# Transformer encoder block: prompt scores in tiles of their own, gates and Fourier map around the attention drain re-ordered, three weight splits and two norms moved

## The chip, the cores and the metric

The kernel runs on one core of one Trainium2 chip. The metric is the device time of one execution in microseconds (us). The traces name the engines PE (TensorE), ACT (ScalarE), DVE (VectorE), POOL (GpSimd) and SP (SyncE, which here issues most of the DMAs).

## The reference

One encoder layer in float32 runs on two batches with shared weights: a prompt of 256 tokens and a sample of 1024 tokens. 16 learned meta tokens stand ahead of each.

```python
h = rms_norm(x, norm_mix_g)
z = h @ w_in            # q | k | v | fourier channels | attention gates | fourier gates
q, k = axial_rope(head_rms_norm(q)), axial_rope(head_rms_norm(k))
a  = bidirectional_gqa(q, k, v) @ w_attn_o      # 8 query heads, 2 key/value heads, softmax over all tokens
fo = fourier_mix(f) @ w_four_o                  # real part of a 2-D DFT over positions and channels
merged = sigmoid(g_attn) * a + sigmoid(g_four) * fo
x = x + merged @ w_out
h2 = rms_norm(x, norm_ffn_g)
gate, up = split(h2 @ w_ffn_in)                 # D_FF = 2816
x = x + (silu(gate) * up) @ w_ffn_out
y = rms_norm(x, final_norm_g)                   # meta tokens dropped
```

`D_MODEL` is 1024, the head width 64. Every linear map is wanted at float32 accuracy.

## The kernel before

**Matmuls in three terms.** Each float32 operand is split into a high part (a cast to the short float type `fp32r`) and a low part (the difference). `three` (lines 228 to 234) issues high x high, high x low and low x high, so one product is a triple of matmuls (L232, L233, L234). A weight block is therefore loaded by DMA, cast on ACT and subtracted on DVE or POOL before PE can use it; that is called its split.

**Chunks.** Tokens are kept in three chunks: chunk 0 and 1 are the halves of the sample (512 columns each), chunk 2 the prompt (256). Tiles 0 to 7 are 128 sample tokens each, tiles 8 and 9 are the prompt's.

**Order of work.** `build` opens PSUM pools one after the other and runs: norm, transposes and first gates; Fourier transform in, q, k and v with the gates of chunk 0; attention with the gates of chunks 1 and 2 as filler; merge; `w_out`; SwiGLU in (`ffn_in`); SwiGLU out (`ffn_out`). Inside a `manual_schedule` region the engines named issue in the order in which the code emits the instructions. Attention names PE, ACT, DVE and POOL, the merge PE, ACT and DVE, the second part of `w_out` only PE. Elsewhere, and on SP, a scheduler places instructions. Each engine works through its queue in order.

**Attention.** `attention` goes over 20 units, a tile and a key/value group each, prompt tiles first: `[8, 9] + list(range(8))`. A unit has four heads. Per head: scores into PSUM tile `S` (L1016), the negated row maximum on DVE (L1021), the exponential with row sum on ACT (L1028), the reciprocal on DVE (L1035). `S` is one tile of three banks (1536 columns). A sample head has a new tile; all prompt heads share one, at thirds of 512 columns:

```python
if S is None or t < 8:
    S = ps.tile([P, 1536], F32, tag=tag_s, name=f"S{t}{g}{h}")
base = 248 if t < 8 else (4 * i + h) % 3 * 512
```

The second half of a unit's work, `Second`, follows one unit later in turns, one per block of 128 keys and one for the meta keys (nine turns for the sample, three for the prompt). A turn transposes four heads' probabilities on PE (L916), splits them on ACT (L927) and DVE (L928), and multiplies with the values (`product`, L949 to L954). After the last turn ACT and DVE copy the two halves of `pv` out (L957, L958), POOL adds them (L959), the row sums come by DMA (L960), POOL multiplies (L963) and a DMA stores the result to `a_d` (L966). What is left of the last units after the last score is called the drain.

**The filler.** Attention is a generator that yields each half step of a head with its kind. `Filler` adds `FILL[kind]` ns for each yield to a debt and pulls gate triples from `gate_gen` until it is paid. A triple of n columns costs 3n/2.4: 640 for chunk 1, 320 for chunk 2; there are 12 units of eight triples for each of both chunks. The kinds are "p" for prompt heads, "first" for the first sample unit, "s" for the other sample units, "end" for the last unit and "drain". The splits of the next gate weights and the copies of gate results wait in a list, `later`, for a slack half step.

**Merge.** `merge` goes over eight blocks `i` of 128 output columns. `load` fetches the block's weights, `need` splits them (two sums on DVE, two casts on ACT, two subtractions on DVE: L1163 to L1168), `load_gates` fetches gates, `sigmoid` applies the sigmoid (L1176). `fourier(i)` computes the Fourier map of the block in two halves (`fo`, L1190 and triples), then the sum and the difference of its two PSUM tiles (`fst`, L1203, L1210, L1211) and the products with the gates on POOL (L1220). Then the attention map of the block runs for chunks 0, 2, 1 (`m`). `load_af` loads one chunk of attention results from `a_d` and splits it (L1119, L216, L217). The final cast and subtraction of a chunk's result are put off in the list `late` (`rows`, L1277 and L1278). Loop order before: `fourier(i + 1)`, then `need(i + 2)`, then the chunks of block `i`.

**w_out and SwiGLU.** `w_out` runs for tiles (0, 2, 1, 3, 8, 9) as `w02` and then for (4, 6, 5, 7) as `w1`; the second half of `w1` goes tile by tile. `h2_norm` makes the second norm of a tile (L249, L241, L242, L254), `second_norm` the seven left operands of a pair of tiles. SwiGLU is computed by seven products `j` for each step `e`; `ffn_units` is a generator that loads, adds and splits their weights (L1477 on ACT, L1479 on POOL in the first two steps, on DVE later). Names in the trace: `i` is a SwiGLU product, `A` and `Ah` its left operands, `w` a split weight, `wo` a `w_out` product.

Of the kernel before, what the change touches and what calls it, by code (L numbers as in the profile page):

```python
# [9 lines left out]
F32 = mybir.dt.float32  # L10
# [7 lines left out]
P = 128  # L18
# [34 lines left out]
FINISH = (1, 3, 5, 7, 9)  # L53
LAG = 6000
FIRST = 4
XLOAD = 3
# [103 lines left out]
class Filler:  # L160
# [5 lines left out]
    def __call__(self, cost):  # L166
        self.debt += cost
        while self.live and self.debt > 0:
            try:
                self.debt -= next(self.gen)  # L170
            except StopIteration:
                self.live = False

    def rest(self):
        if self.live:
            run_all(self.gen)

# [6 lines left out]
class Kernel:  # L184
# [379 lines left out]

    FILL = {"s": 550, "p": 150, "first": 1150, "end": 550, "drain": 600}

# [314 lines left out]
    def attention(self, ps, tiles, tag_s, tag_v):  # L881
# [97 lines left out]

        queue, n, divide, S = deque(), 0, None, None  # L980

# [15 lines left out]
        for i, (t, g) in enumerate(units):  # L997
# [10 lines left out]
            for h in range(4):  # L1008
                hq = q[t][:, (4 * g + h) * P : (4 * g + h + 1) * P]

                if S is None or t < 8:
                    S = ps.tile([P, 1536], F32, tag=tag_s, name=f"S{t}{g}{h}")
                base = 248 if t < 8 else (4 * i + h) % 3 * 512
                for lo, hi in zip(cuts, cuts[1:]):
                    for v in range(2):
                        nc.tensor.matmul(  # L1016
                            S[:, base + lo : base + hi], hq, self.kT[seq][g][v][:, lo:hi], start=v == 0, stop=v == 1
                        )
                sm = self.small.tile([P, 4], F32, tag="sm", name="sm", bufs=4)
                nb = sm[:, 0:1]  # L1020
                nc.vector.tensor_reduce(nb, S[:, base : base + L], axis=AX.X, op=ALU.max, negate=True)  # L1021
# [6 lines left out]
                self.last_exp = nc.scalar.activation(  # L1028
                    p[:, :L], S[:, base : base + L], AF.Exp, bias=nb, accum_out=p[:, L:wide]
                )  # L1030
# [17 lines left out]
            queue.append((Second(i, t, g, ps4, slots), n + 1))  # L1048
        divide()
        while queue:  # L1050
            for half in range(2):
# [78 lines left out]
    def merge(self, then):  # L1130
# [46 lines left out]

        def fourier(i):

# [4 lines left out]
            for half in range(2):  # L1184
                pp = []
                for odd in range(2):
                    pm = self.mm[0].tile([P, 512], F32, tag="out", name=f"fo{i}{half}{odd}")
                    if odd == 0:
# [10 lines left out]
                    pp.append(pm)  # L1199
                while late:  # L1200
                    late.popleft()()
                st = sl.get("fst")
# [5 lines left out]
                for l, n, L, b, c0 in spans:  # L1208
# [6 lines left out]
                    for src, t, n in ((x[:, skip:], l + skip - N_META, n - skip), (d[:, m - 1 :: -1], L - (l + m - 1) - N_META, m)):  # L1215
                        while n:
# [4 lines left out]
                            src, t, n = src[:, k:], t + k, n - k  # L1221
                sl.put(st)
            sl.put(w)

# [9 lines left out]
        need(1)  # L1234
        yield from fourier(0)
        load(2)
        load_gates(2)
        for i in range(8):
            yield from fourier(i + 1)
            if i:  # L1240
                need(i + 2)
            if i == 0:
# [50 lines left out]
    def w_out(self, tiles, ps, then=None, apart=False):  # L1293
# [37 lines left out]
        for half in range(2):  # L1331
# [4 lines left out]
            if half and apart:  # L1336
                need(7)
                next(then)
                for ti, t in enumerate(tiles):
                    for kk in range(4):  # L1340
                        product(acc[ti], t, kk, units[4 + kk])
                        yield 1300
                    add(t, half, acc[ti])
                for kk in range(4):
                    sl.put(*units.pop(4 + kk))
                continue
# [140 lines left out]

    def ffn_in(self, ps, units, side, then):
# [4 lines left out]
        ahead = deque()  # L1493

# [9 lines left out]
        for e, (f, chunks) in enumerate(STEPS):  # L1504
# [3 lines left out]
            for j in range(7):  # L1508
                need(AHEAD - (e < N_EARLY))
                w = ahead.popleft()  # L1510
                for c in chunks:
# [45 lines left out]
                    if e < N_EARLY:  # L1557
                        for _ in range(1):
                            next(side, None)
                sl.put(w)  # L1560
# [209 lines left out]
    def build(self):  # L1770
# [3 lines left out]
        with self.psum("pb", {"mm": 4, "tr": 2, "g": 2}) as ps:  # L1774
# [17 lines left out]
            next(gates.gen)  # L1792
        self.M, self.X, self.af = {}, {}, {}
        ps_e = []
# [3 lines left out]
        m = self.merge(w02)  # L1798
        with self.psum("pd", {"S": (1, 1536), "tr": 2, "pv": 1, "g": 2}) as ps:
            E = mybir.EngineType  # L1800
            self.mm = ps, "g"
            with self.tc.manual_schedule(engines={E.PE, E.Activation, E.DVE, E.Pool}):
                later = self.later = deque()
                parts = self.fourier_parts()
                for i, (kind, more, slack) in enumerate(self.attention(ps, [8, 9] + list(range(8)), "S", "pv")):
# [4 lines left out]
                    if kind == "drain" and not self.af:  # L1810
                        next(m)
                        early = chain(self.load_af(0), self.load_af(2))
                        next(early)
                    gates(self.FILL[kind] + more)
                while later:
                    later.popleft()()
                self.later = None
                run_all(parts)
                gates(2600)
                next(m)  # L1820
                self.last_af = self.load_af(1)
                for i, _ in enumerate(early):
                    gates(2600)
                    if i == 0:
                        next(self.last_af)
                gates.rest()
            self.free_hT(self.hT[1])
            self.free_hT(self.hT[2])
        with self.psum("pe", {"in": 4, "out": 4}) as ps:
            self.mm = ps, "in"  # L1830
            ps_e.append(ps)
# [153 lines left out]
```

## Time and profile before

| | us |
|---|---|
| three runs | 1708.84, 1714.28, 1714.66 |
| their median | 1714.28 |
| the profiled execution | 1710.69 |
| its span in the profile | 1708.8 |
| PE busy | 1645.1 |
| DVE busy | 1096.7 |
| ACT busy | 725.4 |
| POOL busy | 355.8 |

The span is that of the profiled execution, from its first to its last instruction; the time of the same execution is 1.9 us longer. Busy times are of the whole span. A busy engine is not one at full speed: the clock granted to PE is shown for each stretch, 1.00 being full. The stages, read from the first and last instruction of the tiles named:

| stage | from | to |
|---|---|---|
| all ahead of attention | 0 | 316.7 |
| prompt attention (first `S` to first sample `S`) | 316.7 | 355.7 |
| sample attention, to the last head's first half step | 355.7 | 622.8 |
| drain, to the last `pv` | 622.8 | 646.5 |
| rest of gates, Fourier map of blocks 0 and 1, chunks 0 and 2 of block 0 | 646.5 | 673.2 |
| merge from block 0, chunk 1 | 673.2 | 757.5 |
| `w_out` | 757.5 | 874.4 |
| start of SwiGLU | 874.4 | 889.7 |
| SwiGLU in and out, final norm | 889.7 | 1708.8 |

### The profile page before, as it was taken

Reading aid. Unit: us, or ns where it says so; the run is one execution under the profiler, and the core shown is the slowest. Engines: PE = TensorE matmul, PEld = TensorE weight load, DVE = VectorE, ACT = ScalarE, POOL = GpSimd, SP = SyncE. Lnnn points to the kernel's source line nnn. Section 1 sums busy time; section 2 is a strip of 40 time slices with the busy share of each in tenths; the row PEclk is TensorE's granted clock in tenths of the full one; section 3 lists DMA queues with packets and bytes.
Section 4 is the critical chain, followed back from the end, with each engine's and each line's share of the span. In section 5 each row is a group of like instructions: output and inputs, shape, how many; then the busy total and the mean of one; then the engine's idle time right before and its main releaser. Section 6 shows DMA issues by size and latency. Waiting matters only on the chain.

```text
span 1708.8 us, 25999 instructions
## 1 busy us (share of the span) xinstructions
PE 1645.1 (96%) x9739; PEld 1479.5 (87%) x9739; DVE 1096.7 (64%) x2028; ACT 725.4 (42%) x1463; POOL 355.8 (21%) x400
## 2 busy tenths in 40 slices
PE   7999999889999998999989999999999999999997
PEld 7888879668888887778879999999999998888886
DVE  5564565357777665651589667666766778765685
ACT  6423233346666665440454222232222224444444
POOL 3451443222234323661451000000000000000002
PEclk9999999899999999999999999999999999999999
DMA  6135221322122246443522222232223237553534
GB/s 248 44 112 191 99 101 61 105 62 70 52 69 64 78 129 225 136 142 111 197 99 90 96 91 73 84 104 92 84 96 100 84 124 258 200 171 98 164 93 154
DMA packets 92453, 198.75 MB, mean 116 GB/s; under 512 B 10230, under 2 KB 41622, under 8 KB 92328
## 3 DMA queue, kind: packets, MB, share of 16 engines
q1 hardware_dynamic: 82296, 179.63, 31.9%
q10 hardware_dynamic: 8400, 12.53, 2.1%
q0 software_dynamic: 1632, 4.93, 0.9%
q8 instruction: 77, 1.26, 0.3%
q14 instruction: 48, 0.39, 0.1%
HBM read 141.58 MB, written 55.47 MB: 115 GB/s over the span
## 4 chain that ended last, share of the span: by engine, by line
PE 75%; DVE 9%; ACT 5%; issue 4%; POOL 3%; DMA 3%; SPq 0%; ACTq 0%; POOLq 0%; DVEq 0%
PE i L234 10%; PE i L232 10%; PE i L233 10%; PE o L234 5%; PE o L233 5%; PE o L232 5%; PE S L1016 4%; PE pt L916 3%; PE g L234 2%; PE g L232 2%; PE g L233 2%; PE pv L949 2%; PE pv L950 1%; PE wo L233 1%; PE wo L234 1%
## 5 line engine op out<-in xcount | busy, mean ns | idle before, releaser
L1477 ACT CAST w<-wi 128x512 fp32r<-128x512 f32 x168 | 104.0, 621 | 270.9 <-PE i L234 217.4
L232 PE MATMUL i<-A,w 128*128 128x384 f32 x616 | 209.0, 339 | 3.0 <-ACT w L1477 2.6
L234 PE MATMUL i<-A,w 128*128 128x384 f32 x616 | 208.9, 340 | 2.3 <-POOL w L1479 2.3
L233 PE MATMUL i<-A,w 128*128 128x384 f32 x616 | 208.5, 338 | 0.0
L234 PE MATMUL i<-Ah,w 128*128 128x256 f32 x616 | 173.3, 282 | 0.0
L233 PE MATMUL i<-Al,w 128*128 128x256 f32 x616 | 173.3, 281 | 0.0
L232 PE MATMUL i<-Ah,w 128*128 128x256 f32 x616 | 173.2, 281 | 0.0
L241 POOL TENSOR_SCALAR fin0r<-fin0ss 128x1 f32<-128x1 f32 x1 | 0.8, 788 | 755.7 <-ACT X L249 755.7
L1479 DVE TENSOR_TENSOR w<-wi,w 128x512 fp32r<-128x512 f32 x154 | 105.2, 684 | 28.7 <-ACT w L1477 28.1
L232 PEld LDWEIGHTS i<-A,w 128*128 128x128 f32 x616 | 116.9, 190 | 3.6 <-ACT w L1477 2.9
L234 PEld LDWEIGHTS i<-A,w 128*128 128x128 f32 x616 | 116.6, 189 | 3.0 <-POOL w L1479 2.9
L233 PEld LDWEIGHTS i<-A,w 128*128 128x128 f32 x616 | 116.7, 189 | 0.0
L232 PEld LDWEIGHTS i<-Ah,w 128*128 128x128 f32 x616 | 116.0, 188 | 0.5 <-ACT w L1477 0.5
L233 PEld LDWEIGHTS i<-Al,w 128*128 128x128 f32 x616 | 116.3, 189 | 0.0
L234 PEld LDWEIGHTS i<-Ah,w 128*128 128x128 f32 x616 | 116.2, 189 | 0.0
L1021 DVE TENSOR_REDUCE sm<-S 128x1 f32<-128x1040 f32 (+1 forms) x80 | 86.4, 1079 | 35.9 <-PE S L1016 33.0
L928 DVE TENSOR_TENSOR pT<-pt,pT 128x512 fp32r<-128x512 f32 x110 | 75.5, 687 | 51.0 <-ACT pT L927 50.9
L916 PE MATMUL pt<-ident,p 128*128 128x128 f32 (+1 forms) x507 | 90.7, 279 | 0.5 <-DVE hT0l L928 0.4
L927 ACT CAST pT<-pt 128x512 fp32r<-128x512 f32 x110 | 64.1, 583 | 49.7 <-PE pt L916 47.1
L234 PE MATMUL o<-wfo,act 128*128 128x512 f32 (+1 forms) x212 | 82.2, 388 | 2.0 <-DVE act L1611 2.0
L233 PE MATMUL o<-wfo,act 128*128 128x512 f32 (+1 forms) x212 | 81.8, 386 | 0.0
L232 PE MATMUL o<-wfo,act 128*128 128x512 f32 (+1 forms) x212 | 81.6, 388 | 0.0
(841 smaller groups left out, 4563.9 us busy)
## 6 DMA issues: line engine op xcount, KB each, us to landing
wi<-w_fi SPq DMA_DIRECT2D x48, 512.0 KB
act_d<-sc SPq DMA_DIRECT2D x77, 192.0 KB
act<-act_d SPq DMA_DIRECT2D x37, 320.0 KB
wg<-w_g SPq DMA_DIRECT2D x23, 512.0 KB
wfo<-w_fo SPq DMA_DIRECT2D x21, 512.0 KB
X<-act_d SPq DMA_DIRECT2D x31, 320.0 KB
act_d<-sc SPq DMA_DIRECT2D x77, 128.0 KB
gt<-gate SPq DMA_DIRECT2D x32, 256.0 KB
```

The source lines that it names most:

```text
L232: mm(out, sh, mh, start=first and i == 0, stop=False)
L233: mm(out, sh, ml, start=False, stop=False)
L234: mm(out, slo, mh, start=False, stop=last and i == n - 1)
L916: nc.tensor.transpose(pt[:m, h * P : (h + 1) * P], me.ps4[h][:, col : col + m], self.ident[:])
L927: nc.scalar.copy(hi, pt[:rows, :])
L928: nc.vector.tensor_tensor(lo, pt[:rows, :], f32(hi), op=ALU.subtract)
L949: nc.tensor.matmul(me.pv[:], vst, pT[:, :512], start=j == 0, stop=False)
L950: nc.tensor.matmul(me.pv[:], vst, pT[:, 512:1024], start=False, stop=False)
L1016: nc.tensor.matmul(S[:, base + lo : base + hi], hq, self.kT[seq][g][v][:, lo:hi], start=v == 0, stop=v == 1)
L1021: nc.vector.tensor_reduce(nb, S[:, base : base + L], axis=AX.X, op=ALU.max, negate=True)
L1477: nc.scalar.copy(w[:, :512], src)
L1479: eng.tensor_tensor(w[:, 512:1024], src, f32(w[:, :512]), op=ALU.subtract)
```

## The change

- **Prompt scores.** The pool of attention has no `S` any more. `attention` opens a pool of its own for scores: three tiles of 512 columns for the prompt, a new tile for each head; when the sample's first head comes it closes that pool and opens one with a tile of 1536. It closes this one before the drain.
- **Filler.** "s" and "end" go from 550 to 660 and "drain" from 600 to 900. In the drain the filler is no longer the gates but the merge generator, up to the end of `fourier(0)`.
- **Preparation.** A generator, `prepare`, starts when the gates have ended: it flushes `later`, frees the transposed inputs `hT[1]` and `hT[2]`, loads weights and gates of block 0 and the attention columns of chunks 0 and 2, and in the next half steps splits them. Before, this began in the drain, and `fourier(0)` after it. The loads and splits of chunk 1 (`last_af`) stay behind the drain.
- **Merge.** `need(i + 2)` runs after the first half of `fourier(i + 1)` instead of after both. The put-off rows come after the sums of a half, not ahead of its copy. Both steps of the first `w_out` weight (load, split) are taken at block 6; before, the split was at block 7.
- **SwiGLU.** In the last tile of `w1`, after products 0 and 2, a SwiGLU weight is added and split and put in `ahead`, and the `w_out` units are given back one by one. Ahead of `ffn_in` the norms of tiles 4 and 6 are made, those of 5 and 7 in step 0 after products 0 and 2; before, all four came ahead of `ffn_in`.

```diff
-    FILL = {"s": 550, "p": 150, "first": 1150, "end": 550, "drain": 600}
+    FILL = {"s": 660, "p": 150, "first": 1150, "end": 660, "drain": 900}
...
-                if S is None or t < 8:
-                    S = ps.tile([P, 1536], F32, tag=tag_s, name=f"S{t}{g}{h}")
-                base = 248 if t < 8 else (4 * i + h) % 3 * 512
+                n_s, base = (1536, 248) if t < 8 else (512, 0)
+                if banks is None or n_s not in banks:
+                    if banks is not None:
+                        (pool,) = banks.values()
+                        pool.__exit__(None, None, None)
+                    banks = {n_s: self.psum(f"{tag_s}{n_s}", {tag_s: (1536 // n_s, n_s)}).__enter__()}
+                S = banks[n_s].tile([P, n_s], F32, tag=tag_s, name=f"S{t}{g}{h}")
...
         divide()
+        banks[1536].__exit__(None, None, None)
...
-        def fourier(i):
+        def fourier(i, then=None):
...
-                while late:
-                    late.popleft()()
                 st = sl.get("fst")
...
                 sl.put(st)
+                while late:
+                    late.popleft()()
+                if half == 0 and then is not None:
+                    then()
...
         yield from fourier(0)
+        yield None
...
-            yield from fourier(i + 1)
-            if i:
-                need(i + 2)
+            yield from fourier(i + 1, (lambda: need(i + 2)) if i else None)
...
             if i == 6:
                 sl.put(*self.fparts.values(), self.y64)
+                next(then)
                 next(then)
...
-                if c == 0 and i == 7:
-                    next(then)
...
+                        if ti == 3:
+                            sl.put(*units.pop(4 + kk))
+                            if kk in EARLY_W:
+                                self.ahead.append(next(then))
...
+                    if e == 0 and j in (0, 2):
+                        self.h2_norm(PAIRS[4][j // 2 : j // 2 + 1], gf)
...
+                def prepare():
+                    while later:
+                        later.popleft()()
+                    self.later = None
+                    self.free_hT(self.hT[1])
+                    self.free_hT(self.hT[2])
+                    next(m)
+                    early = chain(self.load_af(0), self.load_af(2))
+                    next(early)
+                    yield
+                    next(m)
+                    for _ in early:
+                        yield
...
+                    if kind == "drain" and gates.live:
+                        gates.rest()
+                    if not gates.live:
+                        ahead = ahead or prepare()
+                        next(ahead, None)
+                    if kind == "drain":
+                        first(self.FILL[kind])
                     gates(self.FILL[kind] + more)
...
-            self.h2_norm(CH_TILES[1], gf)
-            sl.put(gf)
+            self.h2_norm(PAIRS[3], gf)
             out = self.ffn_out(ps)
-            self.ffn_in(ps, units, chain(*pairs[3:]), out)
+            self.ffn_in(ps, units, chain(*pairs[3:]), out, self.ahead, gf)
```

More of the change, by code (lines that the diff above doesn't have):

```diff
@@ L54 @@
 LAG = 6000
+EARLY_W = (0, 2)
 FIRST = 4
@@ L168, in __call__ @@
         while self.live and self.debt > 0:
-            try:
-                self.debt -= next(self.gen)
-            except StopIteration:
+            cost = next(self.gen, None)
+            if cost is None:
                 self.live = False
+            else:
+                self.debt -= cost
     def rest(self):
-        if self.live:
-            run_all(self.gen)
+        while self.live:
+            self.live = next(self.gen, None) is not None
 def chain(*gens):
@@ L978, in leaves @@
                 x[0] -= 1
-        queue, n, divide, S = deque(), 0, None, None
+        queue, n, divide, banks = deque(), 0, None, None
         def turns(k):
@@ L1186, in fourier @@
                 for odd in range(2):
-                    pm = self.mm[0].tile([P, 512], F32, tag="out", name=f"fo{i}{half}{odd}")
+                    pm = self.mm[0].tile([P, 512], F32, tag=self.mm[2], name=f"fo{i}{half}{odd}")
                     if odd == 0:
@@ L1238, in merge @@
         for i in range(8):
-            yield from fourier(i + 1)
-            if i:
-                need(i + 2)
+            yield from fourier(i + 1, (lambda: need(i + 2)) if i else None)
+            if i == 7:
+                while late:
+                    late.popleft()()
             if i == 0:
@@ L1342, in w_out @@
                         yield 1300
+                        if ti == 3:
+                            sl.put(*units.pop(4 + kk))
+                            if kk in EARLY_W:
+                                self.ahead.append(next(then))
                     add(t, half, acc[ti])
-                for kk in range(4):
-                    sl.put(*units.pop(4 + kk))
                 continue
@@ L1486, in ffn_units, with ffn_in @@
             sl.put(g)
-    def ffn_in(self, ps, units, side, then):
+    def ffn_in(self, ps, units, side, then, ahead, gf):
         nc, sl = self.nc, self.sl
@@ L1492, in ffn_in @@
         scratch = [(s1[:, 0:384], s1[:, 384:768], s0[:, 0:768], s2[:, 0:768])]
-        ahead = deque()
         def need(n):
@@ L1557, in ffn_in @@
                     if e < N_EARLY:
-                        for _ in range(1):
-                            next(side, None)
+                        next(side, None)
+                    if e == 0 and j in (0, 2):
+                        self.h2_norm(PAIRS[4][j // 2 : j // 2 + 1], gf)
+                        if j:
+                            sl.put(gf)
                 sl.put(w)
@@ L1792, in build @@
             next(gates.gen)
-        self.M, self.X, self.af = {}, {}, {}
+        self.M, self.X, self.af, self.ahead = {}, {}, {}, deque()
         ps_e = []
@@ L1798, in build @@
         m = self.merge(w02)
-        with self.psum("pd", {"S": (1, 1536), "tr": 2, "pv": 1, "g": 2}) as ps:
+        with self.psum("pd", {"tr": 2, "pv": 1, "g": 2}) as ps:
             E = mybir.EngineType
-            self.mm = ps, "g"
+            self.mm = ps, "g", "g"
             with self.tc.manual_schedule(engines={E.PE, E.Activation, E.DVE, E.Pool}):
@@ L1804, in build @@
                 parts = self.fourier_parts()
+                ahead, first = None, Filler(m)
+                def prepare():
[11 more added lines that the diff above has]
+                        yield
                 for i, (kind, more, slack) in enumerate(self.attention(ps, [8, 9] + list(range(8)), "S", "pv")):
@@ L1809, in build @@
                         next(parts, None)
[L1810 to L1813, printed above, removed]
+                    if kind == "drain" and gates.live:
[5 more added lines that the diff above has]
+                        first(self.FILL[kind])
                     gates(self.FILL[kind] + more)
-                while later:
-                    later.popleft()()
-                self.later = None
                 run_all(parts)
-                gates(2600)
-                next(m)
+                run_all(ahead)
                 self.last_af = self.load_af(1)
[L1822 to L1828, printed above, removed]
+                next(self.last_af)
+                first.rest()
         with self.psum("pe", {"in": 4, "out": 4}) as ps:
-            self.mm = ps, "in"
+            self.mm = ps, "in", "out"
             ps_e.append(ps)
```

## The prediction

> **What bounds the kernel now.** I began with the page, at the head and the engines' busy shares.
>
> ```profile
> span 1708.8 us, 25999 instructions
> PE 1645.1 (96%) x9739; PEld 1479.5 (87%) x9739; DVE 1096.7 (64%) x2028; ACT 725.4 (42%) x1463; POOL 355.8 (21%) x400
> ```
>
> TensorE bounds it: only 63.7 us of 1708.8 are not its own. The change removes no matmul, so whatever it wins lies in those 63.7 us and in matmuls run at a lowered clock. Then I cut the span into stages, each row a start and end, the length, the busy us of PE, PEld, DVE, ACT and POOL, the granted clock, DMA share and GB/s.
>
> ```profile
> 316.70:355.70 39.00, 25.94 (x113) 18.88 (x111) 17.45 (x44) 17.02 (x47) 6.36 (x5) 0.82 0.20 67
> 355.70:622.80 267.10, 263.02 (x1625) 227.53 (x1626) 186.19 (x291) 177.93 (x320) 81.78 (x69) 1.00 0.22 66
> 622.80:646.50 23.70, 23.10 (x142) 19.50 (x141) 13.81 (x24) 12.13 (x22) 5.83 (x5) 1.00 0.68 211
> 646.50:673.20 26.70, 19.96 (x111) 18.07 (x110) 14.40 (x24) 15.54 (x26) 12.90 (x16) 0.87 0.72 237
> 673.20:757.50 84.30, 78.00 (x422) 66.85 (x421) 53.62 (x107) 42.59 (x87) 50.74 (x65) 1.00 0.44 144
> 874.40:889.70 15.30, 10.37 (x45) 9.71 (x44) 14.07 (x12) 8.36 (x14) 14.86 (x12) 0.78 0.36 134
> 889.70:937.00 47.30, 46.95 (x297) 46.27 (x296) 46.22 (x76) 21.42 (x41) 9.98 (x7) 1.00 0.24 75
> ```
>
> They are, in order: prompt attention; sample attention up to the last head's first half step; the drain; the time until merge block 0 reaches chunk 1, the first matmul that needs the drain's last product; the rest of the merge; the start of SwiGLU; what follows it. TensorE's idle time is length less busy: 13.1, 4.1, 0.6, 6.7, 6.3, 4.9, 0.4. The stages that the change edits hold nearly all of it.
>
> **Part A, prompt scores in three tiles.** Groups of prompt attention (engine, operation, tile, shape, count | busy, mean ns | idle before, releaser), and two rows in order of time.
>
> ```profile
> L1016 PE MATMUL S<-kTp,qT 128*128 128x272 f32 x32 | 9.3, 377 | 11.8 <-ACT p L1028 11.8
> L1028 ACT ACTIVATE p<-S,sm 128x272 f32<-128x272 f32 x16 | 7.8, 486 | 6.3 <-DVE sm L1021 6.3
> L1021 DVE TENSOR_REDUCE sm<-S 128x1 f32<-128x272 f32 x16 | 7.1, 441 | 15.0 <-PE S L1016 14.5 <-issue 0.2 <-ACT wgh L585 0.2
> L928 DVE TENSOR_TENSOR pT<-pt,pT 128x512 fp32r<-128x512 f32 x5 | 3.5, 692 | 4.0 <-ACT pT L927 4.0
> L927 ACT CAST pT<-pt 128x512 fp32r<-128x512 f32 x5 | 2.9, 586 | 7.3 <-PE pt L916 7.3
> L920 DVE COPY ao<-pt 17x512 f32<-17x512 f32 x3 | 2.0, 682 | 0.4 <-PE pt L916 0.3
> L927 ACT CAST mt<-pt 16x512 fp32r<-16x512 f32 x3 | 1.7, 574 | 6.3 <-DVE ao L920 6.3
> L958 DVE COPY ao<-pv 64x512 f32<-64x512 f32 x2 | 1.4, 680 | 0.0
> 342.03 0.19 ACT L1028 ACTIVATION_READ_ACCUMULATOR p<-S,sm 128x1 f32 x1
> 342.27 0.52 PE L1016 MATMUL S<-kTp,qT 128*128 128x272 f32 x2 [1.02 <-ACT p L1028]
> ```
>
> All prompt heads share one tile, in thirds one bank wide. Yet a head's scores start 0.05 us after the exponential of the head before has ended (342.03 + 0.19, then 342.27), though that lies in another third: the wait goes by tile. With three tiles a head waits only for the third head before it. Next to be late is the pair ScalarE and VectorE, which hand each other the transposed probabilities. In a unit that runs its three turns I sum what must alternate: two casts and subtractions, 2 x (0.586 + 0.692) = 2.6; a reduction, the row-sum copy, the meta cast and a subtraction, 0.441 + 0.682 + 0.574 + 0.692 = 2.4; one exponential between them, 0.486 + 0.19 = 0.7; two copies out of pv, 0.586 + 0.680 = 1.3. That is 6.9, and I take 7.4 for gate casts queued on ScalarE. Three such units are 22.1. The first has no turns: four exponentials, 2.7, a pair of score matmuls, 0.5, a reduction, 0.4, and a microsecond of gate work: 4.6. Together 26.7 for 39.0: **-12.3**. Bounds: 0 if the wait only changes its name; -21.6 if VectorE's 17.45 busy us alone are left.
>
> The skill speaks against this gain. The Trainium skill, "PSUM — Partial Sum Buffer", section "PSUM bank collisions raise a hardware error", has PSUM guarded by bank and quadrant; by that rule the old thirds, in banks of their own, were free of each other already, and the sum would lack its 12.3. The trace disagrees: 0.05 us behind the exponential is a wait for it.
>
> **Part B, fill of 660 for 550.** The filler counts 12 units of 8 x 640 + 8 x 320 ns: 92,160. Its credits up to the last attention unit are some 5,400 in the prompt, 9,200 in the first sample unit and 112 half steps of 550, now 660: 76,200 before, 88,500 after. So the gates now end in the last unit's third head, where before 27 of 192 triples were still to come: 16 in the drain, 11 behind it. Gates from 622.6 on, then the first and the last matmul of those eleven.
>
> ```profile
> L234 PE MATMUL g<-hT1h,wgl 128*128 128x512 f32 x12 | 4.7, 393 | 0.0
> L234 PE MATMUL g<-hT2h,wgl 128*128 128x256 f32 x16 | 4.5, 282 | 0.0
> 646.40 0.40 PE L232 MATMUL g<-hT1h,wgh 128*128 128x512 f32 x1
> 651.19 0.28 PE L234 MATMUL g<-hT2h,wgl 128*128 128x256 f32 x1
> ```
>
> Eleven triples (3 wide, 8 narrow, a narrow one being half) take 4.9 us, 0.70 for a wide one. Of the 12 + 16 shown one wide one came earlier, so 11 + 8 = 19 are moved, 13.3 us. Sample attention grows by as much, since PE is busy 263.0 of its 267.1 us: 0 in the sum (at best its 4.1 idle us take some), and what the gates leave uncovered is part C.
>
> **Part C, Fourier block 0 in the drain.** What VectorE gets there, and the chain behind the last pv.
>
> ```profile
> 647.83 0.41 DVE L1163 TENSOR_TENSOR wmf<-wmf 128x256 f32<-128x256 f32 x1
> 648.49 0.68 DVE L1168 TENSOR_TENSOR wm<-wmf,wm 128x512 fp32r<-128x512 f32 x1
> L217 DVE TENSOR_TENSOR afl<-af,afh 128x1024 fp32r<-128x1024 f32 x2 | 2.4, 1223 | 0.5 <-ACT afh L216 0.5
> L1210 DVE TENSOR_TENSOR fst<-fst,fo 128x328 f32<-128x328 f32 (+2 forms) x6 | 2.3, 378 | 2.3 <-PE fo L234 2.3
> L216 ACT CAST afh<-af 128x1024 fp32r<-128x1024 f32 x3 | 3.0, 1043 | 6.1 <-DMA a_d<-ao 5.7 <-ACT gs L592 0.4
> 647.98 2.94 POOL L959 TENSOR_TENSOR ao<-ao 64x512 f32<-64x512 f32 x1 [7.04 <-DVE ao L958]
> 650.94 3.57 DMA ao<-rc_d
> 654.64 1.29 POOL ao L963
> 655.95 2.45 DMA a_d<-ao
> tabc<-pos_c POOLq DMA_DIRECT2D x4, 520.0 KB, 4.2
> ```
>
> Into the drain come two weight splits (two adds and two subtractions, 2.2 each), three splits of attention columns (3.7) and the sums and differences of one Fourier block (2.3, half of the x6 and as much for L1211). With the 13.81 of the stage row VectorE has 24.2. PE has 23.1 less 16 triples (8.4) plus a Fourier block of 25 matmuls, 3.9: 18.6. VectorE bounds it, and in order: I take 25, between 21.5 (some of its work slips behind the last turn) and 32 (splits wait for their loads). Behind the last pv, 1.4 for two copies, 1.3 on GpSimd (2.9 in the row, beside VectorE), 3.6, 1.3, 2.5, then a 512 KB load, 4.2 by the nearest row, and cast and subtraction, 2.3: 16.5. The PE work to lay over it is Fourier block 1 and chunks 0 and 2 of block 0, 3.9 + 4.2, so 8 us stand open and the clock falls: 2 us more. Together 43.5. Before, the two stages took 50.4, without the moved gates 37.1: **+6.4**, from -4 to +14. The preparation's 21 SP issues (weights, gates, attention columns) come earlier by some half steps of the drain; what their queue can do is the third rival.
>
> The clock: in the row 646.50 the granted clock is 0.87 beside 6.7 idle us. The Trainium skill, "TensorE: Matmul & The Clock Gate", section "Part 1: The HAM clock gate", gives half rate after an idle window of about 3.4 us and full rate after as much work; the trace agrees. By it the 2 us would go only if the gap of 8 fell under that window, and the sum would be 2 better.
>
> **Part D, merge.** Waits of TensorE in the merge (us in all, times, longest).
>
> ```profile
> PE fo L232 <- ACT wm L1167: 2.3, 3, 0.8
> PE wo L232 <- ACT woh L216: 1.7, 1, 1.7
> ```
>
> These and their like (the low parts, a block whose weights sit in another slot) are the stage's 6.3 idle us. Splitting the next weights after half 0 puts them half a block, some 5 us, earlier; their load was issued a block earlier still (84.3 / 8 = 10.5), so it covers 4.2 twice. The w_out split moves a block earlier, right behind its load: it can hold up sigmoids and rows behind it on ScalarE by 0 to 4.2 us, with half of that engine's time free. I take **-5.8**; bounds 0 and -6.3.
>
> **Part E, start of SwiGLU.** Two waits, a norm, and the clock there.
>
> ```profile
> 880.13 0.44 PE L232 MATMUL i<-A,w 128*128 128x384 f32 x1 [2.64 <-ACT w L1477]
> 883.39 0.69 PE L234 MATMUL i<-A,w 128*128 128x384 f32 x1 [2.29 <-POOL w L1479]
> 873.29 2.31 DVE L254 SCALAR_TENSOR_TENSOR h<-X,n25r,norm_ffn_g 128x1024 f32<-128x1024 f32 x1 [0.38 <-POOL n25r L242]
> 883.00:889.00 6.00, 5.61 (x17) 5.61 (x18) 6.00 (x5) 2.96 (x5) 6.00 (x5) 0.50 0.00 0
> ```
>
> The weights of products 1 and 2 are late behind norms: 4.9 idle us, and 2.7 at half clock (883 to 889, 5.6 busy). Splitting two weights during w_out and putting two norms off takes both waits. But VectorE is then the bound for a while: 14.07 of 15.3, then 46.22 of 47.3, and the norms (2.31) stay in that stretch. Half comes back: **-3.5**, from 0 to -7.6.
>
> **Sum.** -12.3 + 0 + 6.4 - 5.8 - 3.5 = -15.2. The profiled execution took 1710.7, so 1695.5. The median of the three runs, 1714.3, is 3.6 above it; a measurement of this kernel tells about 0.5%, 8.6 us, from no change. I say 1697, which leaves part of that offset.
>
> **Rivals.** First one row of SP's waits (us in all, times, longest) in the second half of sample attention, the drain and after, for the third.
>
> ```profile
> SPq L960 <- POOL ao L959: 27.4, 6, 7.0
> ```
>
> 1. All parts pay and the drain costs nothing: the gates' room is filled, VectorE's 24.2 falls beside other waits. For it: PE's 0.6 idle in the drain before. Against: the 16.5 chain with 8 us over it. Then C is -2, E -7.6: 1710.7 - 27.7 = 1683.
> 2. The scores don't come free: prompt attention stays bound by ScalarE and VectorE handing over, 15.0 idle us of the reductions turning into waits for casts. A gives 0 to -3: 1705 to 1708. The rule of the PSUM page would lead here. Against: 11.8 of TensorE's 13.1 idle us name the exponential.
> 3. Slower: the preparation's splits stand at the head of ScalarE and VectorE while SP is held by the drain's own transfers. SP's longest wait for GpSimd's sum is 7.0; three splits that wait that long are 21, and with 2.7 of half clock for each, as in part E, 29: 1724.5. It decides from 27.4 us on, since 1695.5 + 27.4 is 1722.9. Against: the loads need nothing that the drain makes, and at 4.2 each they fit into its 25 several times.
>
> **How the numbers follow.** The forecast has 0.46 (1688 to 1704 by the bounds of C and E), the first rival 0.24, the second 0.16 (half of it within 0.5%, that is above 1705.7), the third 0.08 (half of it slower than 1722.9), the rest 0.06. Faster by over 0.5%: 0.77; within: 0.17; slower: 0.06. The range leaves out the third rival and what lies beyond the first: 1682 to 1710.
>
> **What would show it.** A: prompt attention at 27 us, scores no longer waiting for the exponential, the clock above 0.82. B: no gate matmul in the drain, sample attention 13 longer. C: VectorE full in the drain, and 8 us open before chunk 1 of block 0. D: no wait of fo for wm. E: no wait over 1 us for w. Wrong if the drain exceeds 32, or if prompt attention stays over 33.

## The result and the profile after

The changed kernel takes 1702.64 us (median of four runs, 1701.7 to 1703.62) against 1712.55 for the kernel before in the runs that go with it: ratio 0.9945, 95% interval 0.9924 to 0.9966. It is faster by about 0.55%, by the interval between 0.34 and 0.76%. The forecast was 1697 within 1682 to 1710. The number held; two of its five terms, C and E, did not.

First the head of the page and the same stages as before. Columns: start and end, length, busy us of PE, PEld, DVE, ACT, POOL, granted clock, DMA share, GB/s.

```profile
span 1699.9 us, 25999 instructions
PE 1638.0 (96%) x9739; PEld 1480.4 (87%) x9739; DVE 1100.9 (65%) x2028; ACT 725.0 (43%) x1463; POOL 350.9 (21%) x400
...
316.90:340.30 23.40, 17.69 (x112) 15.11 (x110) 16.09 (x44) 16.48 (x47) 6.37 (x5) 0.98 0.31 109
340.30:618.30 278.00, 275.27 (x1705) 242.45 (x1706) 185.87 (x290) 179.75 (x323) 83.73 (x70) 0.99 0.24 74
618.30:652.90 34.60, 22.31 (x120) 17.92 (x119) 23.22 (x40) 21.04 (x36) 7.36 (x10) 0.85 0.53 179
652.90:668.30 15.40, 9.78 (x58) 8.62 (x57) 4.05 (x9) 3.61 (x6) 6.11 (x9) 0.95 0.71 224
668.30:746.80 78.50, 77.50 (x415) 67.79 (x416) 52.24 (x102) 41.27 (x85) 46.16 (x62) 0.97 0.37 121
867.80:883.10 15.30, 12.73 (x71) 12.30 (x71) 13.52 (x12) 7.38 (x13) 13.64 (x12) 0.89 0.28 101
883.10:930.40 47.30, 45.45 (x286) 44.43 (x285) 46.80 (x80) 21.87 (x41) 9.05 (x6) 1.00 0.24 79
```

The end of one stage is another instruction here. The prediction cut at the first matmul of chunk 1 in merge block 0 (673.2) and took 757.5 for the start of `w_out`. In the changed kernel the first half of that chunk, which needs only the other key/value group, starts at 661.1, so the rows above cut at its second half and at the first `w_out` matmul. Cut in the same way, the kernel before has:

```profile
646.50:674.50 28.00, 21.26 (x116) 19.15 (x115) 15.43 (x26) 15.78 (x27) 13.30 (x16) 0.88 0.69 227
674.50:756.20 81.70, 76.20 (x415) 65.58 (x413) 51.29 (x102) 41.88 (x87) 50.34 (x64) 1.00 0.44 143
```

Row by row: the prompt fell from 39.0 to 23.4; sample attention grew from 267.1 to 278.0; the drain grew from 23.7 to 34.6; the way to the second half of chunk 1 fell from 28.0 to 15.4; the rest of the merge fell from 81.7 to 78.5. So the prompt and the merge pay, and the gates moved into sample attention and the longer drain take most of it back.

One more cut tells what need not be looked at. From the first `w_out` matmul to the end of the span the kernel before took 952.6 us (1708.8 - 756.2) and the changed one 953.1 (1699.9 - 746.8). By the same subtraction all kernels below lie between 950 and 955, whatever they do at the start of SwiGLU. What moved the time by more than these 5 us lies ahead of `w_out`; a smaller difference can lie on either side, and one below lies behind it.

### The profile page after: what moved, and what is told of

Its sections match the earlier page's. It is cut to its first block, busy times and chain, and to the rows that moved or that the text cites. A ratio compares the mean times of both kernels' runs of the same rounds, so it can differ in the third digit from the quotient of the medians.

```text
span 1699.9 us, 25999 instructions
## 1 busy us (share of the span) xinstructions
PE 1638.0 (96%) x9739; PEld 1480.4 (87%) x9739; DVE 1100.9 (65%) x2028; ACT 725.0 (43%) x1463; POOL 350.9 (21%) x400
## 4 chain that ended last, share of the span: by engine, by line
PE 49%; DVE 4%; POOL 3%; DMA 2%; issue 2%; ACT 2%; POOLq 0%; SPq 0%; DVEq 0%; ACTq 0%
PE i L237 9%; PE i L235 9%; PE i L236 9%; PE o L237 5%; PE o L236 5%; PE o L235 5%; PE wo L236 1%; PE wo L235 1%; PE wo L237 1%; POOL gt L1284 1%; POOL wol L220 1%; DMA wo<-w_out 1%; POOL w L1492 0%; DVE wi L1471 0%; DMA wi<-w_fi 0%
## 5 line engine op out<-in xcount | busy, mean ns | idle before, releaser
L931 DVE TENSOR_TENSOR pT<-pt,pT 128x512 fp32r<-128x512 f32 x121 | 83.1, 687 | 54.9 <-ACT pT L930 53.7
L930 ACT CAST pT<-pt 128x512 fp32r<-128x512 f32 x121 | 70.6, 583 | 58.2 <-PE pt L919 50.2
```

Source lines behind the costliest of these rows:

```text
L930: nc.scalar.copy(hi, pt[:rows, :])
L931: nc.vector.tensor_tensor(lo, pt[:rows, :], f32(hi), op=ALU.subtract)
```

## The experiments

All kernels were timed in five rounds beside the kernel before on the same chip. From here on, A to E are the parts as the prediction names them. A table of what came out, then each with its edit.

| kernel | median us | ratio to before, 95% interval |
|---|---|---|
| A | 1696.4 | 0.9917, 0.9903 to 0.9931 |
| A + D | 1688.3 | 0.9870, 0.9855 to 0.9886 |
| A + D + E | 1689.9 | 0.9878, 0.9862 to 0.9894 |
| A + B + D | 1690.4 | 0.9883, 0.9869 to 0.9897 |
| A to E, the change | 1702.6 | 0.9945, 0.9924 to 0.9966 |

### A alone

```diff
-                if S is None or t < 8:
-                    S = ps.tile([P, 1536], F32, tag=tag_s, name=f"S{t}{g}{h}")
-                base = 248 if t < 8 else (4 * i + h) % 3 * 512
+                n_s, base = (1536, 248) if t < 8 else (512, 0)
...
+                S = banks[n_s].tile([P, n_s], F32, tag=tag_s, name=f"S{t}{g}{h}")
```

> Only part A, prompt scores in three one-bank tiles, put on the kernel before; fill, drain, merge, w_out and SwiGLU stay as they were. Ledger theory (the stages of the two traces add up, one part each): prompt attention about 23.5 us as after the whole change (it was 39.0), but sample attention starts behind 2.5 us of idle TensorE at half clock and loses 2 to 3 of it again, so 12.5 to 15 us faster than before, some 1698. Rival: the sample attention behind it is bound by something that starts with the prompt (gate weights, the q loads), so that it takes back most: under 5 us faster.

Measured: 1696.4, 14.6 us less than the 1711.0 beside it. Prompt attention is 23.4 us, as in the whole change. TensorE's waits in it (us in all, times, longest):

```profile
PE S L1020 <- ACT p L1032: 2.5, 1, 2.5
PE pt L916 <- ACT p L1032: 2.4, 2, 1.3
PE pt L916 <- DVE pT L928: 0.8, 1, 0.8
```

Of the 11.8 us that scores waited for the exponential one wait is left, 2.5 us at the first sample score, whose tile takes all three banks. The wait went by tile, as the two rows of the prediction said; A is worth what the ledger theory expected. The program makes that wait itself, by a semaphore (its PSUM pools are opened with `reuse_waits="tile"`), so it tells how this program guards a tile; how the banks behave no run here tests.

### A and D

```diff
-            yield from fourier(i + 1)
-            if i:
-                need(i + 2)
+            yield from fourier(i + 1, (lambda: need(i + 2)) if i else None)
...
+                next(then)
```

The put-off rows and the first `w_out` weight move too, as in the whole change.

> Parts A and D (merge order and the first w_out weight), nothing else of the change. Ledger theory: another 4 to 5 us faster than part A alone, as the rest of the merge fell from 83.1 to 78.5 between the traces, some 1694. Rival: the merge gained only because Fourier block 0 had been done in the drain, and with the old drain the new order does nothing: within 1.5 us of part A alone.

Measured: 1688.3, 8.1 us less than A alone, more than the 4 to 5 expected. TensorE's waits from chunk 1 of block 0 to the first `w_out` matmul, in A and then in A + D:

```profile
PE fo L232 <- ACT wm L1172: 2.2, 3, 0.8
PE wo L232 <- ACT woh L216: 1.7, 1, 1.7
PE fo L232 <- ACT ml L1172: 0.7, 1, 0.7
PE fo L234 <- DVE wm L1173: 0.6, 4, 0.2
PE fo L234 <- DVE ml L1173: 0.2, 1, 0.2
```

```profile
PE fo L234 <- DVE wm L1173: 0.3, 2, 0.2
PE fo L232 <- ACT wm L1172: 0.3, 2, 0.2
PE fo L234 <- DVE ml L1173: 0.2, 1, 0.2
```

From 5.4 us to 0.8; the stretch fell from 83.1 to 77.1 us. The old drain is still there, so the rival (the merge gains only through the Fourier block in the drain) is out.

### A, D and E, and a third weight

```diff
+                            if kk in EARLY_W:
+                                self.ahead.append(next(then))
...
+            self.h2_norm(PAIRS[3], gf)
```

> Parts A, D and E (early SwiGLU weights, two norms put off): the whole change without the higher fill and without the new drain. Ledger theory: B and C cost 8 to 10 us net, so this is 8 to 10 us faster than the whole change, some 1693; against A and D it is within 1.5 us, since w_out lost 3.1 and SwiGLU won 2.6. Rival: B and C feed the parts behind them, and the kernel without them is no faster than the whole change, 1702.

Measured: 1689.9, 1.5 above A + D with intervals that overlap: E is worth nothing that can be told, and B and C cost 12.8 us together. The second run set `EARLY_W` to (0, 1, 2):

> Parts A, D and E with three SwiGLU weights split ahead instead of two. With two the wait for a weight at the start of SwiGLU did not go: 4.8 us in four waits for 4.9 in two. Theory one, it moved to the third weight, and a third one ahead takes 2 to 3 us of it: 1687. Theory two, GpSimd's subtractions and VectorE's additions and norms bound the first steps, so that it moves on again: within 1.5 us of two weights, 1690.

Measured: 1690.2, as with two. TensorE's largest waits in the 62.6 us from the first SwiGLU matmul, with none, two and three weights ahead (A + D, A + D + E, the third):

```profile
PE i L232 <- ACT w L1484: 2.6, 1, 2.6
PE i L234 <- POOL w L1486: 2.3, 1, 2.3
```

```profile
PE i L235 <- POOL w L1489: 3.5, 2, 2.6
PE i L233 <- ACT w L1487: 1.3, 2, 0.8
```

```profile
PE i L233 <- DVE sg L1538: 5.0, 1, 5.0
PE i L233 <- DVE sc L1541: 1.8, 1, 1.8
```

The waits are 4.9, 4.8 and 6.8 us and have another name each time: the high part of a weight, then GpSimd's low part, then a sum on VectorE that frees a tile. They do not go, they move. The same 62.6 us in A + D, in A + D + E and with three weights (columns as in the stages):

```profile
851.83:914.43 62.60, 57.28 (x341) 55.97 (x340) 60.30 (x87) 29.77 (x54) 24.93 (x18) 0.95 0.27 89
```

```profile
851.00:913.60 62.60, 57.49 (x349) 55.93 (x348) 60.33 (x88) 30.07 (x56) 23.64 (x19) 0.97 0.25 81
```

```profile
852.27:914.87 62.60, 55.71 (x335) 54.53 (x334) 57.85 (x85) 29.85 (x55) 22.89 (x20) 0.95 0.24 81
```

VectorE is busy 60.3 of 62.6 us in the first two: E changes the order of its work and not its amount. That VectorE bounds this stretch is the likely reading and not shown: no run took work off it there, and with three weights TensorE waits longest while VectorE is busy 57.9 us.

### A, B and D

```diff
-    FILL = {"s": 550, "p": 150, "first": 1150, "end": 550, "drain": 600}
+    FILL = {"s": 660, "p": 150, "first": 1150, "end": 660, "drain": 600}
```

> Parts A and D with the higher fill of part B (660 for 550), the drain and all behind it as before. Parts B and C together cost 12.8 (1702.6 for the whole change, 1689.9 without them). Theory one, taking the filler away is what costs: sample attention grows by the 11 that it grew by in the whole change, and of the 13.3 us of gates missing in and behind the drain only a half is saved, since the chain behind the last pv then lies open: 5 to 9 us slower than A and D, 1693 to 1697. Theory two, the work put into the drain is what costs and the fill is neutral: within 2 us of A and D, 1688.

Measured: 1690.4, 2.1 above A + D, a tenth beyond theory two and well below theory one. Sample attention grew by 9.6 us, from the first sample score to the last score 269.7 to 279.3, and from the last pv to the first `w_out` matmul 8.0 came back, 103.6 to 95.6. The row that matters is the drain, from the last score to the last pv, in the kernel before and then in A + B + D:

```profile
624.40:646.06 21.66, 21.06 (x131) 17.73 (x129) 13.31 (x22) 10.54 (x19) 5.09 (x4) 1.00 0.70 219
```

```profile
620.54:642.42 21.88, 14.72 (x85) 10.52 (x86) 15.40 (x24) 13.38 (x24) 3.83 (x3) 1.00 0.74 239
```

TensorE lost 6.3 us of work there and the length stayed near 21.8. So the amount of TensorE's work, 21.1 of 21.7, is not what gives this drain its length. TensorE's largest wait in A + B + D points at the hand-over: TensorE transposes, ScalarE casts, VectorE subtracts, and that frees the tile for the next transposes.

```profile
PE pt L916 <- DVE pT L928: 3.6, 3, 1.7
```

The two rows differ in one thing more. In A + B + D the split of the first merge weight is done inside the drain, and sigmoids with it: VectorE has 2.1 us more and ScalarE 2.8, and the drain is not longer for it. Whether it would be shorter without them no run shows.

So C is what costs: against A + B + D the whole change has 12.2 us more, of which E may hold 1.5.

### What in C costs: four edits of the whole change

In the drain of the changed kernel TensorE waits twice for long. A first edit put the splits two half steps further from their loads:

```diff
                     next(early)
                     yield
+                    yield
+                    yield
                     next(m)
```

> The whole change, with the splits of the preparation two half steps later than their loads (two bare steps more in the generator that prepares). Theory: TensorE's 5.8 us wait in the drain is ScalarE standing at the head of its queue for the load of the attention columns, with VectorE behind it; two half steps are 3 to 4 us, and 3 to 6 us come back: 1697 to 1700. Rival: VectorE's work sets the drain (19.0 busy of 28.9, and the later splits meet the Fourier sums), so the wait moves to another instruction: within 1.5 us of the whole change.

Measured: 1703.5, the rival. The second, on top, gave the Fourier block tiles that wait for nobody:

```diff
+                    own = i == 0 and not (half and odd)
+                    pool, tag = (self.fo, "out") if own else (self.mm[0], self.mm[2])
```

> The whole change with the late splits of the run before (two half steps behind their loads) and PSUM tiles for the Fourier block in the drain that wait for nobody: three banks that the scores have left, and one gate bank. Theory one, TensorE's 7.9 us wait there is the reuse of the two gate banks, with the copy that frees them late on ScalarE: the wait goes and the drain is 5 to 8 us shorter, 1696 to 1698. Theory two, ScalarE and VectorE, in order, set the drain: the wait moves to the transposes, whose tiles the same two engines free, and the time stays within 2 us of the whole change.

Measured: 1703.3, theory two. TensorE's largest waits between last score and last pv, in the change, with late splits, and with late splits and own tiles:

```profile
PE pt L919 <- DVE afl L931: 5.8, 1, 5.8
PE fo L1198 <- ACT fst L1209: 4.2, 1, 4.2
```

```profile
PE fo L1198 <- ACT fst L1209: 7.9, 1, 7.9
```

```profile
PE pt L919 <- DVE pT L931: 5.5, 3, 4.3
PE pt L919 <- DVE mt L931: 3.0, 1, 3.0
```

Ten us went to eight and to eight and a half, and the drain was 32.8, 32.5 and 32.2 us: neither the load nor the tiles alone set its length. The next two edits were to take work out of the drain instead:

```diff
-        need(1)
         yield from fourier(0)
         yield None
+        need(1)
```

> The whole change, with the weight split of block 1 issued behind the drain instead of in it. VectorE gets 10.4 us of added work in the drain (two weight splits at 2.2, three attention splits at 1.23, one Fourier block's sums and differences 2.3), and the drain grew by 10.9 against A, B and D. Theory, the hand-over of ScalarE and VectorE sets the drain and added work comes on top in full: 2.2 less, 30.6 us from the last score to the last pv for 32.8, and 1 to 2 us of it in the total: 1701. Rival, single stalls set it (the load that the first attention split waits for): 32.8 as before, 1702.6.

```diff
                     next(m)
-                    for _ in early:
-                        yield
+                    yield
+                    self.early = early
...
+                for k, _ in enumerate(self.early):
```

> The whole change, with the three attention splits issued behind the drain. Theory, added work comes on top in full: 3.7 us less, 29.1 us from the last score to the last pv; behind the drain VectorE was busy 4 of 15.4 us, so most of the 3.7 shows in the total: 1699 to 1700. Rival, the load that the first attention split waits for is the cost: its 5.8 us wait of TensorE goes with it, 26 to 27 us from the last score to the last pv and 1696.

Measured: 1699.2 with the edit of the weight split and 1696.2 without the attention splits in the drain, 3.4 and 6.5 us less than the change. The drain of the change, of the one and of the other:

```profile
619.92:652.69 32.77, 21.02 (x112) 17.07 (x112) 22.23 (x37) 19.77 (x34) 7.36 (x10) 0.84 0.55 184
```

```profile
620.76:650.81 30.05, 20.10 (x111) 15.98 (x112) 21.31 (x35) 19.65 (x34) 7.92 (x10) 0.89 0.58 188
```

```profile
619.81:648.43 28.62, 20.37 (x111) 16.68 (x111) 18.72 (x34) 16.71 (x31) 7.37 (x10) 0.88 0.63 198
```

The lengths came within 0.6 us of what the theory expected, 30.1 for 30.6 and 28.6 for 29.1. They do not confirm it, since the work was not what the theory took. The first edit did not put the weight split of block 1 behind the drain. Its sums ran ahead of the last score (at 620.76), its casts and subtractions still in the drain (`wmf` and `wma` hold the raw weight of block 1 here):

```profile
611.80 0.42 DVE L1171 TENSOR_TENSOR wmf<-wmf 128x256 f32<-128x256 f32 x1
612.14 0.42 DVE L1172 TENSOR_TENSOR wmf<-wmf 128x256 f32<-128x256 f32 x1
638.14 0.63 ACT L1175 CAST afl<-wmf 128x512 fp32r<-128x512 f32 x1
638.96 0.68 DVE L1176 TENSOR_TENSOR afl<-wmf,afl 128x512 fp32r<-128x512 f32 x1
643.18 0.62 ACT L1175 CAST wm<-wma 128x512 fp32r<-128x512 f32 x1 [0.52 <-PE fo L236]
644.27 0.68 DVE L1176 TENSOR_TENSOR wm<-wma,wm 128x512 fp32r<-128x512 f32 x1
```

So VectorE lost 0.9 us of its 22.2 there and not 2.2, ScalarE 0.1, and yet the drain is 2.7 us shorter: where the pieces stand may count too. And A + B + D, against which the added work was counted, has one weight split in its own drain. By the busy time in the rows the change, the first and the second kernel have 6.8, 5.9 and 3.3 us more on VectorE than A + B + D, and 6.4, 6.3 and 3.3 more on ScalarE; they are 10.9, 8.2 and 6.7 us longer. The drain grew by more than either engine got, and by no more than about what both got together. That added work comes on top in full is not shown. Two more things lie in these lengths that no run separates: ScalarE's 2.1 us wait for the load of the first attention column (in the change), and the lower clock, 0.84 to 0.89 for 1.00. The Fourier block, the third of the added parts, was not measured alone: the one kernel planned with it behind the drain gave no time.

What is shown most directly is the second edit. It takes 3.5 us off VectorE and 3.1 off ScalarE in the drain, and the drain is 4.2 us shorter. In the total the rival came nearer, with 1696 to the theory's 1699 to 1700; but the runs of this kernel spread from 1693.0 to 1699.2, and the profile is of the slowest. There the way from the first score to `w_out` is 428.0 us, 1.9 less than the change's 429.9. For the first edit that way is 429.9 too, so nothing was won ahead of `w_out`: in the profiles its gain lies in `w_out` itself, 116.0 us without a wait for 121.1, where TensorE waits 1.9 us for the low part of a `w_out` weight. Why that wait is gone stays open.

### Three tries behind the drain

The first puts the attention splits behind Fourier block 0, in A + D:

```diff
         yield from fourier(0)
+        for k, _ in enumerate(self.early):
+            if k == 0:
+                next(self.last_af)
...
+                self.early = early
```

> Parts A and D, and one new edit in place of B and C: the splits of the attention columns of chunks 0 and 2 are issued behind Fourier block 0 instead of ahead of it; gates stay behind the drain as filler. Theory: TensorE's 6.1 us wait behind the drain (Fourier block 1 for the copy that frees its tile) is ScalarE standing at the split of attention columns, whose slot waits for the last store of the drain; with the copy ahead of it the wait goes and 3 to 6 us come back: 1682 to 1685. Rival: the chain from the last pv to chunk 1 of block 0 ends the stretch in any order: within 1.5 us of A and D, 1688.

Measured: 1694.2, 5.9 us slower than A + D, which neither theory had. ScalarE's first instruction behind the drain that needs a new slot, in A + D and in this kernel (start, duration, engine, line, idle before):

```profile
644.39 1.04 ACT L216 CAST afh<-af 128x1024 fp32r<-128x1024 f32 x1 [5.85 <-DMA a_d<-ao]
```

```profile
645.82 0.62 ACT L1172 CAST wm<-wmf 128x512 fp32r<-128x512 f32 x1 [6.72 <-DMA a_d<-ao]
```

It is another instruction, held by the same store: slots are handed out oldest first, and the next one asked for is that of the last unit's attention output. Now the weight of block 1 got it, and all splits came behind. The other two tries keep that slot back, in A + D and in A + B + D. They also issue the rest of the gates at once and give the slots of the transposed inputs back ahead of the splits:

```diff
-                sl.put(ao)
+                (self.kept if (t, g) == units[-1] else sl).put(ao)
...
-                gates(2600)
+                gates.rest()
+                self.free_hT(self.hT[1])
+                self.free_hT(self.hT[2])
```

> Parts A and D; behind the drain the slots of the transposed inputs are given back as soon as the gates have been issued, and the slot of the last unit's attention output only after the splits that follow. Slots are taken oldest first, and in three runs the first split behind the drain was held 5.7 to 6.7 us by the last store, since it got that slot. Theory: without it Fourier block 1 follows at once and 3 to 6 us come back: 1682 to 1685. Rival: the chain from the last pv (two copies, sum, row sums, product, store, load, split: 16 us) to the second half of chunk 1 ends the stretch anyway, and the wait only moves there: within 1.5 us of A and D, 1688.

> The same slot edit on A, B and D (fill of 660, no gates behind the drain). There is 4.9 us less matmul work to lay over the chain behind the last pv than in the run beside it. Theory: the chain is the bound here, and it stays at 1690, within 1.5 us of A, B and D. Rival: the slot wait (3.7 us) is what ends last here too, and it gains 3 us or more: 1687.

Measured: 1688.8, as A + D, and 1694.0, 3.6 above A + B + D. In the first the wait for the store is gone and the way from the last pv to chunk 1 fell from 26.5 to 23.4 us; the rest of the merge and `w_out` took 1.1 and 4.3 more, with 4.2 less behind. The rival was right on the time, but what ate the 3 us is not settled. The second had nothing to win: A + B + D holds no instruction behind the drain that waits for that store, and the 3.7 us that I had put down to the slot are TensorE's wait for the cast of a weight, which itself waits for VectorE's sums. Neither theory had a loss. Up to `w_out` the kernel is not longer than A + B + D (418.7 and 420.2 us from the first score), the rest is 3.3 us longer (954.6 for 951.3), and why stays open.

The fastest kernels, A + D and the one with the slot kept back, take 1688.3 and 1688.8: some 14 us less than the change.

## Why the prediction was right or wrong

- **A, -12.3 predicted, -14.6 measured.** Right in mechanism, a little small. I summed a unit as one chain of both engines, 7.4 us. The stage came out at 23.4 for 26.7, with ScalarE and VectorE busy 16.5 and 16.1 of it: more of the chain overlapped than I let it.
- **B, 0 predicted, +2.1 measured.** Right within what can be told. Moved work was paid where it went, 9.6 us for the 13.3 that I took, and 8.0 came back behind the drain. At equal clock (last section) the 9.6 are about 9.
- **C, +6.4 predicted, 10.7 to 12.2 measured** (the change less A + B + D, with and without E's 1.5). The sign was right, and the step that failed is the drain's length: "VectorE bounds it, and in order: I take 25". I read TensorE's 23.1 of 23.7 as the old bound and let VectorE's 24.2 us of work replace it, as if an engine could be filled to the brim. The work was sized well, 23.2 us; but the stage came out at 34.6, beyond the 32 that I had named as wrong, with VectorE busy two thirds of it. As I read it now, the old drain is a hand-over of about 22 us between TensorE's transposes, ScalarE and VectorE, with TensorE's filler lying in its gaps. The work of C made it longer by more than either engine got. How much of that is the amount of work, its order, the wait for a load or the clock stays open. The chain behind the last pv came out near its 16.5, at 15.4, and the gap before the second half of chunk 1 at 5.6 us for 8.
- **D, -5.8 predicted, -8.1 measured.** Right: the waits that were named went, 5.4 us to 0.8. The 1.8 us beyond the bound of -6.3 lie within the two intervals.
- **E, -3.5 predicted, nothing measured** (+1.5, overlapping). The prediction had the reason in hand, "VectorE is then the bound for a while", and took half of the gain in spite of it. With 46.22 of 47.3 us busy right behind, the value to take was the bound 0, if that reason is the right one.
- **The sum.** -15.2 predicted; -14.6 + 2.1 - 8.1 + 1.5 + 10.7 is -8.4, and the medians of the change's own runs differ by 9.9. A and D gave 4.6 more than predicted, B, C and E took 11.4 more. The range held because the misses were of both signs and the bounds of C were wide; that the time fell within 6 us of the forecast was luck.
- **The rivals.** The third had the place right, splits standing at the head of ScalarE in the drain, and its price wrong: ScalarE waits once for such a load, 2.1 us where I took three times 7, and the drain costs about 11 us instead of 29. The first, that the drain costs nothing, and the second, that scores don't come free, are out.

## What to carry to other kernels

A stretch where an engine is busy 97% of the time need not be bound by it: take work off that engine there, and see whether the stretch gets shorter. Where in-order engines hand each other every item, work added to them can lengthen the stretch by more than either's share, here 10.9 us for 6.8 and 6.4, and neither later splits nor more tiles helped. Moving work is no gain by itself: attention splits moved behind the drain took 6.5 us off the change, and moved further, behind Fourier block 0, they made A + D 5.9 us slower. When a wait keeps its size and changes the instruction it is shown at, look for what all of them wait for. And read in the trace that an edit moved what it was meant to move, before its time is read.

## What the runs showed of the hardware

After the same 2.5 us wait at the first sample score the clock of TensorE was not the same in every execution. The first 6 us behind that score, in A and in the change:

```profile
340.70:346.70 6.00, 5.88 (x38) 5.09 (x39) 2.60 (x5) 1.72 (x3) 1.28 (x1) 1.00 0.23 55
```

```profile
340.33:346.33 6.00, 6.00 (x24) 5.67 (x25) 1.66 (x4) 1.22 (x2) 1.27 (x1) 0.52 0.16 44
```

Full clock and 38 matmuls in the one, half clock and 24 in the other; in the profiles of the thirteen kernels with prompt tiles of their own two ran there at 1.00 and eleven at 0.50 to 0.75. A and A + D have the same code up to there, and A + D shows 0.72. In the records of all these profiles the granted clock is 0.50 or 1.00 and nothing between, and a stretch at 0.50 lasts 3.4 us or a multiple of it (but for the last, which the end cuts off): 0.72 is one such stretch in 6 us, 0.52 is most of one of 6.8. What it costs can be read from sample attention (first sample score to last score, us). The thirteen kernels run it with two fills, and those of one fill have the same code there but for the preparation in its last half steps:

| half clock at the first sample score | fill 550 | fill 660 |
|---|---|---|
| none | 268.3 | 277.2 |
| 3.4 us | 269.1, 269.7, 269.7 | 278.3, 278.5 |
| 6.8 us | 270.6, 270.6 | 279.3, 279.4, 279.6, 279.9 |

Beside its own length such a gap costs nothing, about 1 or about 2 us, by chance. That is as much as some of the differences above, so one profile of each kernel does not tell them apart.

The Trainium skill, "TensorE: Matmul & The Clock Gate", section "Part 1: The HAM clock gate", has the gate watch a window that runs freely, so that where a gap falls in it is left to chance; the rows agree with that. That page of the Trainium skill asks for at least one idle window, about 3.4 us, before the clock falls; here 2.5 us of idle TensorE were enough, and the measurement decides. The prediction had the trace agree: its row at 646.50 does, where the clock fell in a gap of 6.1 us, but its rows of part E do not, where it fell to 0.50 at gaps of 2.64 and 2.29 us.
